# A two-layer decoder trunk on one Trainium2 core: the last down-weight sums of a layer are made behind the fourth product of pair 10 instead of behind pair 9

## The chip, the cores and the metric

The kernel runs on one core of one Trainium2 chip. Its time is the device time of one execution in microseconds (us), as the median of several runs. The engines of the core work side by side, each through its own queue in order: TensorE (PE, matrix products, with its weight loads as PEld), VectorE (DVE, elementwise work), ScalarE (ACT, elementwise work, casts, and it issues some transfers), GpSimd (POOL) and SyncE (SP, here only an issuer of transfers). They wait for one another through semaphores. [...]

## What is computed

A trunk of two layers on 512 tokens of width 1024. Layer one mixes tokens by pooling, layer two by differential attention; each is followed by a SwiGLU block with 2816 hidden columns, and both parts by a normalization:

```python
def _swiglu(x, w_gate, w_up, w_down):
    return (jax.nn.silu(x @ w_gate) * (x @ w_up)) @ w_down

    for i in range(DEPTH):
        ...
        x = _layernorm(ALPHA * x + h, ln_mix_g[i], ln_mix_b[i])
        x = _layernorm(ALPHA * x + _swiglu(x, w_gate[i], w_up[i], w_down[i]), ln_ffn_g[i], ln_ffn_b[i])
```

Only the SwiGLU block, which runs once in each layer (`ffn`, lines 570 to 1154), has to do with the change.

## The kernel before

**Precision.** Every matrix is split into a high part (a cast on ACT) and a low part (the rest, a subtraction on DVE), and a product is three matmuls: high by high, high by low, low by high. In the trace `g_65h` and `g_65l` are the two parts of a gate or up weight tile, `d_3h` and `d_3l` those of a down weight tile, and `raw` and `r` the tiles as loaded, before the split.

**Fewer products.** The hidden columns are taken in blocks of 128: 22 blocks, numbered so that block k and block k + 11 make pair k. For the pairs of the list `SPLIT` (2 to 10), gate and up are computed together by a fast scheme that needs seven products of half-size operands in place of eight (function `strassen`). Its products are named P1, Q5, P6, Q3, P7, P2 and Q4, and run in that order on TensorE, 24 matmuls each. They use three banks: A collects P1, P6, P7 and Q4, C collects Q5 and Q3, and B holds a copy of A after P1 and then collects P2. Between the products the banks are read:

- after P1, ACT copies A to B (L1015)
- after Q5, ACT copies C to the hidden tile `hid` (L1017); Q3 then adds into C, so it waits for that copy
- after P6, ACT copies A to `hid` (L1019); P7 then adds into A
- after Q3, DVE subtracts with C (L1024)
- after P7, DVE subtracts with A (L1026); Q4 then adds into A, so it waits for that subtraction
- after P2 and Q4, ACT takes the silu of B and A (L1042, L1031), and DVE multiplies (L1044, L1045)

**The down weights and their sums.** The down product is computed by the same kind of scheme, so it needs sums of blocks of the down weights. They are made ahead, one set of terms for each k from 0 to 10, while the pairs run. For a set of terms, POOL issues two loads (L823) and then a third load that accumulates onto the first (L824); this is `load_terms`. Later `weight_sums` makes two additions on DVE (L829, L830), and at the next `catch_up` two transfers issued on ACT (L834) store the four sums in the array `tsum` in memory. In the down product SP loads them back (`r<-tsum`, L612). The tile `b` is one of the buffers of these terms; `b_10` is that of the last set.

**What sets the order.** The program is written out in order; each engine runs its instructions in the order of the code. A unit of the list `ORDER` is a plain block (f) or a fast pair (p). Behind each product of a fast pair the code splits weights ahead of need (`ahead`), issues the stores of sums made earlier (`catch_up`), and then, if the tag of that product stands in the tuple `SUMMED`, makes the next set of sums (`weight_sums`). A tag without a product, such as `p9`, means behind the whole unit. So each of the eleven tags in `SUMMED` is the place of one set of sums, and the stores of a set are issued behind the product that comes next. Behind pair 10 comes the down product, whose items are cast and split on ACT and DVE in the gaps of pair 10. Lines 264 and 265 (`affine`) apply the scale and shift of the previous normalization to one block of `res`.

Of the kernel before, what the change touches and what calls it, by code (L numbers as in the profile page):

```python
# [49 lines left out]
EARLY = (1, 0)  # L50
PRE = SPLIT[:2]
SUMS = {1: (2, 1), 2: (2, 1)}
SUMMED = ("f1", "f2", "f3", "p3", "p4", "p5P2", "p6P7", "p7P7", "p8P6", "p9Q5", "p9")
EAGER = 6
GB = "p3"
MORE = True
# [22 lines left out]
def trunk(ctx, tc, x, wall, pscale, lam_p, subln, table, lng, lnb, band, first, onehot, out):  # L79
# [490 lines left out]
    def ffn(layer, late):  # L570
# [7 lines left out]
        with tc.tile_pool(name=f"ffn{layer}", bufs=1) as fp:  # L578
# [264 lines left out]
            def weight_sums():  # L843
                g = sum_terms(summed_rows[0])
                summed_rows[0] += 1
                next(g)
                behind.append(g)
# [4 lines left out]
            def catch_up():  # L852
                for g in list(behind):
                    if next(g, g) is g:
                        behind.remove(g)
# [139 lines left out]
            def strassen(k):  # L995
# [10 lines left out]
                for p in BEGUN if begun else GATE:  # L1006
# [30 lines left out]
                    if not (k == PRE[0] and p == "Q5"):  # L1037
                        catch_up()
                    if f"p{k}{p}" in SUMMED:
                        weight_sums()  # L1040
# [7 lines left out]
            for kind, i in units(layer):  # L1048
                (plain if kind == "f" else strassen)(i)
                unit = f"{kind}{i}"  # L1050
                if unit in SUMMED:
                    weight_sums()
# [636 lines left out]
```

## Time and profile before

| | us |
|---|---|
| median of 3 runs | 935.93 |
| the runs | 937.68, 929.84, 935.93 |
| the profiled execution's own time | 932.08 |
| its span, first to last instruction | 930.3 |

The profile has the span and the busy time of each engine, the waits (which instruction waited for which), the chain of work that ended last, and timelines. A row of a timeline gives the start in us from the span's start, the duration in us, the engine, the line of the kernel, the operation, the tiles it writes and reads, and, in brackets, the idle time of the engine ahead of it and what ended it. ACTq and SPq are the queues of ACT and SP where they issue transfers. A matmul is recorded with its start; the ends are modelled and overlap the next start, so the pace of a product is read from the starts. The granted clock of TensorE was 0.998 of full speed in this execution.

### The profile page before, as it was taken

To read this page: it belongs to the slowest core of one execution; us is meant where nothing else is said; L and a number is where in the kernel's file an instruction comes from. 1 tells how busy PE (TensorE), PEld (TensorE's weight loads), DVE (VectorE), ACT (ScalarE), POOL (GpSimd) and SP (SyncE) were. 2 spreads that over 40 slices of the span, in tenths; PEclk is the share of its full clock that TensorE was granted. 3 is DMA by queue.
4 is the path that set the end of the run, shared out by engine and by line. 5 is a ranking of instruction groups with operands and counts; after the bars stand their busy time and mean duration, and the time that the engine had idled before them with its cause. 6 is when DMAs were issued, how large, how long until landed. Compare 5 with 4: busy or idle time off the path is not lost. (4 is left out here: it accounts for less than half of the span.)

```text
span 930.3 us, 15038 instructions
## 1 busy us (share of the span) xinstructions
PE 917.7 (99%) x5806; PEld 826.9 (89%) x5806; DVE 803.9 (86%) x1163; ACT 529.0 (57%) x841; POOL 110.4 (12%) x129
## 2 busy tenths in 40 slices
PE   9999999999999999999999999999999999999996
PEld 8999999999988888878888888989999999988885
DVE  7998798998889998868989786877798999889988
ACT  6773354544555557676878854843454444555551
POOL 4121121110100001201111100201111110100001
PEclk9999999999999999999999999999999999999999
DMA  8397888877656688976664622468878887756653
GB/s 222 130 296 227 291 253 248 261 248 236 219 194 201 193 238 236 226 194 163 158 148 113 156 92 72 158 227 259 263 195 291 266 262 226 229 185 204 192 204 102
DMA packets 72518, 192.50 MB, mean 207 GB/s; under 512 B 14548, under 2 KB 14804, under 8 KB 72446
## 3 DMA queue, kind: packets, MB, share of 16 engines
q1 hardware_dynamic: 44572, 121.36, 39.6%
q0 software_dynamic: 15712, 46.93, 22.4%
q10 hardware_dynamic: 12162, 23.25, 6.7%
q8 instruction: 45, 0.74, 0.3%
q14 instruction: 27, 0.22, 0.1%
HBM read 166.33 MB, written 25.19 MB: 206 GB/s over the span
## 5 line engine op out<-in xcount | busy, mean ns | idle before, releaser
L713 DVE TENSOR_TENSOR raw<-raw,raw 128x1024 f32<-128x1024 f32 x52 | 63.3, 1221 | 0.7
L160 DVE TENSOR_TENSOR xs<-hid,xs 128x512 fp32r<-128x512 f32 x84 | 53.5, 639 | 0.0
L159 ACT CAST xs<-hid 128x512 fp32r<-128x512 f32 x84 | 48.6, 581 | 0.4 <-DVE hid L1044 0.4
L1322 ACT ACTIVATE p<-p,mn 128x128 f32<-128x128 f32 (+3 forms) x64 | 35.3, 552 | 14.1 <-DVE mn L1317 14.1
L823 POOL DMA_DIRECT2D b<-in_wall x24 | 17.9, 793 | 141.5 <-DMA tsum<-b 35.1
L1317 DVE CUSTOM_DVE_ANT_0 p<-s,bias 128x128 f32<-128x128 f32 (+3 forms) x64 | 28.0, 485 | 1.1 <-PE s L1302 1.1
L823 POOL DMA_DIRECT2D hid<-in_wall x20 | 15.0, 751 | 114.0 <-DVE hid L829 28.6
L1017 ACT COPY hid<-C 128x512 f32<-128x512 f32 x18 | 10.6, 587 | 29.1 <-PE C L919 14.3
L1024 DVE TENSOR_TENSOR hid<-C,hid 128x512 f32<-128x512 f32 x18 | 12.4, 690 | 16.4 <-PE C L919 13.4
L235 POOL TENSOR_TENSOR rs<-rs,mhalf 128x1 f32<-128x1 f32 x16 | 12.5, 782 | 102.7 <-DVE rs L234 95.7
L286 ACT ACTIVATE y<-pt,bT,gT 128x128 f32<-128x128 f32 x40 | 15.0, 455 | 15.9 <-PE pt L272 15.8
L226 DVE BATCH_NORM_STATS2 st<-res 128x6 f32<-128x512 f32 x32 | 22.2, 694 | 1.1
L1019 ACT COPY hid<-A 128x512 f32<-128x512 f32 x18 | 10.6, 586 | 20.4 <-PE A L919 20.4
L824 POOL DMA_DIRECT2D b<-in_wall x12 | 14.8, 1230 | 59.7 <-DMA b<-in_wall 59.7
L1031 ACT ACTIVATE sg<-A 128x512 f32<-128x512 f32 x18 | 10.7, 596 | 19.0 <-PE A L919 19.0
L1026 DVE TENSOR_TENSOR hid<-hid,A 128x512 f32<-128x512 f32 x18 | 12.3, 681 | 10.6 <-PE A L919 10.6
L1336 DVE SCALAR_TENSOR_TENSOR p<-p,sm,p 128x128 f32<-128x128 f32 (+3 forms) x32 | 17.6, 552 | 1.1
L713 DVE TENSOR_TENSOR more<-more,raw 128x1024 f32<-128x1024 f32 x15 | 18.3, 1220 | 0.2
L1042 ACT ACTIVATE sg<-B 128x512 f32<-128x512 f32 x14 | 8.3, 593 | 15.3 <-DVE hid L830 6.2
L265 DVE TENSOR_TENSOR res<-res,gb 128x512 f32<-128x512 f32 (+1 forms) x20 | 16.0, 799 | 0.7
L777 ACT CAST xs<-hid 128x1024 fp32r<-128x1024 f32 x8 | 8.4, 1052 | 14.3 <-DVE hid L786 8.7
L160 POOL TENSOR_TENSOR sql<-sq,sqh 128x512 fp32r<-128x512 f32 x7 | 9.3, 1325 | 60.5 <-ACT sqh L159 60.5
(1237 smaller groups left out, 3590.6 us busy)
## 6 DMA issues: line engine op xcount, KB each, us to landing
raw<-in_wall SPq DMA_DIRECT2D x120, 512.0 KB, 5.7
r<-tsum SPq DMA_DIRECT2D x40, 512.0 KB, 4.0
b<-in_wall POOLq DMA_DIRECT2D x36, 512.0 KB, 6.3
hid<-in_wall POOLq DMA_DIRECT2D x30, 512.0 KB, 6.1
r<-in_wall SPq DMA_DIRECT2D x30, 512.0 KB, 4.0
tsum<-b ACTq DMA_DIRECT2D x24, 512.0 KB, 3.8
tsum<-hid ACTq DMA_DIRECT2D x20, 512.0 KB, 5.6
more<-in_wall SPq DMA_DIRECT2D x10, 512.0 KB, 7.0
```

Source lines behind the costliest of these rows:

```text
L159: nc.scalar.copy(dst_h, src)
L160: (low or nc.vector).tensor_tensor(dst_l, src, dst_h.bitcast(F32), op=ALU.subtract)
L226: nc.vector.bn_stats(stats[n, s][:, d, :], res[:, s, d * 512 : (d + 1) * 512])
L235: nc.gpsimd.tensor_tensor(rs, rs, mhalf, op=ALU.pow)
L265: nc.vector.tensor_tensor(z, z, gb[:, 1, c], op=ALU.add)
L286: nc.scalar.activation(y[:, k, :], pt[:, k * P : (k + 1) * P], AF.Identity, bias=bT[:, n, kk : kk + 1], scale=gT[:, n, kk : kk + 1],)
L713: tt(t, raws[pair[0]], raws[pair[1]], op=ALU.add)
L823: nc.gpsimd.dma_start(out=t[:, j], in_=src[:, j])
L824: nc.gpsimd.dma_start(out=t[:, 0], in_=src[:, :, 1], accum_op=ALU.add)
L1317: nc.vector.tensor_tensor_reduce(out=p, in0=accs[c], in1=biases[h][:, w - 1 :: -1] if w < S else biases[h][:, ::-1], op0=ALU.add, op1=ALU. ...
L1322: nc.scalar.activation(p, p, AF.Exp, bias=mn[:, q, c : c + 1], scale=-1.0, accum_out=sm[:, q, c : c + 1],)
L1336: nc.vector.scalar_tensor_tensor(p0[:, r], p0[:, r], sm[:, q, 0:1], p1[:, r], op0=ALU.mult, op1=ALU.add)
```

## The change

One tag of the tuple `SUMMED` is another: the eleventh set of sums (the one of `b_10`) is made behind the product Q3 of pair 10, the fourth of its seven, in place of behind pair 9. The change acts in both layers.

```diff
 EARLY = (1, 0)
 PRE = SPLIT[:2]
 SUMS = {1: (2, 1), 2: (2, 1)}
-SUMMED = ("f1", "f2", "f3", "p3", "p4", "p5P2", "p6P7", "p7P7", "p8P6", "p9Q5", "p9")
+SUMMED = ("f1", "f2", "f3", "p3", "p4", "p5P2", "p6P7", "p7P7", "p8P6", "p9Q5", "p10Q3")
 EAGER = 6
 GB = "p3"
 MORE = True
```

The instructions on each engine are the same in number and kind. On DVE, at the border of pair 9 and pair 10 in the first layer (the numbers behind the names are those of buffers), the row before was:

```order
 L850 TENSOR_TENSOR hid_534<-hid_534 128x256
-L829 TENSOR_TENSOR b_10_2642<-b_10_2642 128x512
-L830 TENSOR_TENSOR b_10_2642<-b_10_2642 128x512
 L264 TENSOR_TENSOR res<-res,gb_1386 128x512
 L265 TENSOR_TENSOR res<-res,gb_1386 128x512
```

The two sums no longer stand between the last work of pair 9 (L850) and the scale and shift of `res`. On DVE in pair 10 of the same layer, the row now is, from the subtraction with bank C behind Q3:

```order
L1024 TENSOR_TENSOR hid_534<-C_10_2782,hid_534 128x2x256 [waits PE_49]
L160 TENSOR_TENSOR d_1l<-r_1_2713,d_1h 128x1024 [waits DMAHW1_49,Activation_49]
L160 TENSOR_TENSOR xs_535<-hid_534,xs_535 128x512 [waits Activation_49]
L829 TENSOR_TENSOR b_10_2642<-b_10_2642 128x512 [waits DMAHW0_49,DMAHW6_49,DMASW7_49,DMASW0_49]
L830 TENSOR_TENSOR b_10_2642<-b_10_2642 128x512 [waits DVE_49]
L1026 TENSOR_TENSOR hid_534<-hid_534,A_10_2781 128x2x256 [waits PE_49]
L160 TENSOR_TENSOR d_2l<-r_2_2808,d_2h 128x1024 [waits DMAHW2_49,Activation_49]
```

They stand there ahead of the subtraction with bank A (L1026); before, L1026 followed the split of `xs` directly. On ACT, the row before, from the copy of bank A to B behind P1 of pair 10:

```order
L1015 COPY B_3_679<-A_10_2783 128x512 [waits PE_49,Activation_49]
L834 DMA tsum_536<-b_10_2642 128x2x512 [waits DMAHW3_49,DMASW0_49]
L834 DMA tsum_536<-b_10_2642 128x2x512 [waits DMASW7_49,DVE_49]
L1017 COPY hid_534<-C_10_2784 128x2x256 [waits PE_49]
L1019 COPY hid_534<-A_10_2783 128x2x256 [waits PE_49]
```

and on ACT now, from the same copy on:

```order
L1015 COPY B_3_679<-A_10_2781 128x512 [waits PE_49,Activation_49]
L1017 COPY hid_534<-C_10_2782 128x2x256 [waits PE_49]
L1019 COPY hid_534<-A_10_2781 128x2x256 [waits PE_49]
L159 CAST d_0h<-r_0_2637 128x1024 [waits DMAHW7_49]
L159 CAST xs_535<-hid_534 128x512
L159 CAST d_1h<-r_1_2713 128x1024 [waits DMAHW1_49]
L159 CAST xs_535<-hid_534 128x512
L159 CAST d_2h<-r_2_2808 128x1024 [waits DMAHW2_49,PE_49]
L159 CAST xs_535<-hid_534 128x512
L834 DMA tsum_536<-b_10_2642 128x2x512 [waits DMAHW6_49,DMASW0_49]
L834 DMA tsum_536<-b_10_2642 128x2x512 [waits DMAHW0_49,DMASW7_49,DVE_49]
L159 CAST d_3h<-r_3_2836 128x1024 [waits DMAHW3_49,PE_49]
```

The two stores moved from ahead of the copy of bank C (L1017) to behind the casts for the third down item, ahead of the cast of `d_3h`; the second of them waits for the sums on DVE.

## The prediction

> **What bounds the kernel now.** I read the page first, then the waits of TensorE, then the chain of work that ended last, and at the place that the chain names the timelines of TensorE, DVE and ACT.
>
> The page's head and the row of its part 1 (busy us, share of the span, instructions):
>
> ```profile
> span 930.3 us, 15038 instructions
> PE 917.7 (99%) x5806; PEld 826.9 (89%) x5806; DVE 803.9 (86%) x1163; ACT 529.0 (57%) x841; POOL 110.4 (12%) x129
> ```
>
> TensorE is the bound nearly everywhere: 930.3 - 917.7 = 12.6 us of the span are without a matmul. A change that leaves the matmuls alone can win only from those. The waits of TensorE (us in total, times, the longest) and of its weight loads say what the idle time in the middle waits for:
>
> ```profile
> PE C L919 <- ACT hid L1017: 2.6, 2, 1.7
> PE pt L272 <- DVE res L244: 0.2, 1, 0.2
> ```
> ```profile
> PEld C L919 <- ACT hid L1017: 3.0, 2, 1.9
> ```
>
> There is one wait of size, twice, once in each layer: a matmul into bank C waits for the copy of bank C by ACT (L1017). The matmuls on either side, from TensorE's timeline (start us, us, operation; idle time before and its releaser in brackets), first layer then second:
>
> ```profile
> 248.48 0.28 PE L919 MATMUL A<-xs,g_66l 128*128 128x256 f32 x1
> 250.45 0.50 PE L919 MATMUL C<-xs,g_67h 128*128 128x256 f32 x2 [1.69 <-ACT hid L1017]
> 250.79 0.28 PE L919 MATMUL C<-xs,g_67l 128*128 128x256 f32 x1
> 804.81 0.28 PE L919 MATMUL A<-xs,g_66l 128*128 128x256 f32 x1
> 806.02 0.50 PE L919 MATMUL C<-xs,g_67h 128*128 128x256 f32 x2 [0.93 <-ACT hid L1017]
> 806.36 0.28 PE L919 MATMUL C<-xs,g_67l 128*128 128x256 f32 x1
> ```
>
> g_66 is the third product of pair 10 (P6), g_67 the fourth (Q3). Why the copy is late stands in the chain of work that ended last (start us, us, what):
>
> ```profile
> 796.89 6.55 DMA b<-in_wall
> ...
> 803.52 0.70 DVE b L829
> ...
> 804.25 0.70 DVE b L830
> ...
> 804.97 0.37 ACTq L834
> ...
> 805.38 0.59 ACT hid L1017
> ...
> 806.02 3.13 PE C L919 x24
> 809.15 2.88 PE A L919 x24
> ...
> 877.66 45.02 PE P L1079 x198
> ```
>
> Read downwards: the accumulating transfer of the last down-weight terms lands at 803.44; the two sums (L829, L830) come after it; the store of the sums (L834) is issued on ACT's queue after them; ACT's copy of bank C stands behind that store; TensorE waits for the copy. A product is 24 matmuls in 2.88 us, 0.12 each. From 806 on the chain is TensorE alone to the last normalization. So these sums, with nothing urgent about them, hold TensorE in each layer.
>
> **The change part by part.** Nothing is added or removed: two sums on DVE and two stores on ACT go from ahead of pair 10 to behind its fourth product, in both layers.
>
> *What the old place gives back.* Layer one: the Q3 matmul was due at 248.48 + 0.12 = 248.60 and started at 250.45, 1.85 late; its first two took 250.79 - 250.45 = 0.34 where 0.24 is the pace, 0.10 more. Layer two: due at 804.93, started at 806.02, 1.09, and again 0.10. Sum 1.95 + 1.19 = 3.14 us. [...]
>
> I take 3.14, from starts, since a start is recorded and an end is modelled; the ends for the range are 2.6 and 3.2.
>
> *Is the copy then in time?* It needs only bank C's product Q5 (ended 802.2 by the pace) and TensorE needs it at 804.93. The store, the only thing that held it, is gone: slack some 2 us.
>
> *What the sums cost in the new place.* Now they stand on DVE just ahead of L1026 (the subtraction that reads bank A after P7), and the first Q4 matmul, which writes into bank A again, waits for L1026. That is the one place where the change can lose, so I laid out DVE and ACT there with the rows of layer two (layer one first, for the same wait; then DVE, then ACT):
>
> ```profile
> 247.95 0.69 DVE L829 TENSOR_TENSOR b<-b 128x512 f32<-128x512 f32 x1 [3.95 <-DMA b<-in_wall]
> ```
> ```profile
> 799.91 0.42 DVE L850 TENSOR_TENSOR hid<-hid 128x256 f32<-128x256 f32 x1
> 803.52 0.69 DVE L829 TENSOR_TENSOR b<-b 128x512 f32<-128x512 f32 x1 [3.19 <-DMA b<-in_wall]
> ...
> 804.86 0.68 DVE L264 TENSOR_TENSOR res<-res,gb 128x512 f32<-128x512 f32 x1
> ...
> 807.32 1.22 DVE L719 TENSOR_TENSOR g_70l<-raw,g_70h 128x1024 fp32r<-128x1024 f32 x1
> 808.46 1.22 DVE L160 TENSOR_TENSOR d_0l<-r,d_0h 128x1024 fp32r<-128x1024 f32 x1
> ...
> 810.20 0.68 DVE L1024 TENSOR_TENSOR hid<-C,hid 128x512 f32<-128x512 f32 x1
> 810.80 1.22 DVE L160 TENSOR_TENSOR d_1l<-r,d_1h 128x1024 fp32r<-128x1024 f32 x1
> ...
> 812.53 0.68 DVE L1026 TENSOR_TENSOR hid<-hid,A 128x512 f32<-128x512 f32 x1
> ```
> ```profile
> 805.86 0.59 ACT L1019 COPY hid<-A 128x512 f32<-128x512 f32 x1
> 806.34 1.06 ACT L159 CAST d_0h<-r 128x1024 fp32r<-128x1024 f32 x1
> ...
> 809.27 1.06 ACT L159 CAST d_2h<-r 128x1024 fp32r<-128x1024 f32 x1
> ...
> 811.95 1.05 ACT L159 CAST d_3h<-r 128x1024 fp32r<-128x1024 f32 x1 [1.10 <-PE A L919]
> ```
>
> DVE after L850 goes straight on: L264 at about 800.25, and g_70l ends (807.32 + 1.22 - 804.86 = 3.68 later) at 803.9. It then waits for d_0h. On ACT, L1019 comes after P6's last matmul ends, 804.81 + 0.28 = 805.09, so at 805.13; d_0h 0.48 behind it at 805.61, ended 806.67. DVE then keeps its old distances: d_0l 806.70, L1024 1.74 later at 808.44, d_1l at 809.04, and 1.73 behind it, at 810.77, the place of L1026. There the sums go in: L829 and L830 take up 804.86 - 803.52 = 1.34, so L1026 runs from 812.11 to 812.79. TensorE, unheld, starts Q4 at 804.93 + 3 x 2.88 = 813.57. Slack 0.78 us, and the same in layer one, whose rows have the same distances from Q3 on. So L1026 costs nothing while that slack stands; if it is gone, each us beyond it is lost once in each layer. Bounds: 0 and, had the sums their whole 1.34 us uncovered, 1.34 - 0.78 = 0.56 a layer. I take 0, nearest to the rows.
>
> *Will the accumulated terms be there?* The landing row of L824's transfers, SP's row of the loads that read the sums, the sixth of them alone, and the landing row of L834's stores:
>
> ```profile
> DMA to landing us min/median/max: 5.7/7.3/12.9
> ```
> ```profile
> 812.04 18.08 SPq L612 DMA_DIRECT2D r<-tsum  x8
> ```
> ```profile
> 824.66 0.32 SPq L612 DMA_DIRECT2D r<-tsum  x1
> ```
> ```profile
> DMA to landing us min/median/max: 2.8/4.0/11.2
> ```
>
> Issued at 796.89, the slowest of its kind (12.9) would land at 809.8, before 810.77; the one seen took 6.55. Wait gone.
>
> *The stores on ACT.* The first waits for nothing that is late and is issued behind d_2's two casts, near 810.1; the second waits for L830, until 812.2, and takes 0.37. d_3h stands behind it: 812.6 in place of 811.95 less the gain, some 1.8 us later against TensorE. Its user is the fourth item of the down products: they start at 813.57 + 2.88 = 816.45, an item has 12 matmuls of 45.02 / 198 = 0.227, so 816.45 + 3 x 2.73 = 824.6. Ten us of cover. Behind it on ACT stand the two silus: the first could run at 813.8 and runs behind d_3's casts at 814.1, the second waits for Q4 as before. 0.
>
> *The stores and who reads them.* The first read of the last terms is the sixth of the loads from tsum, 824.66 less the gain of 1.19, 823.5; the first store, issued at 810.1, lands at 814 by the median and at 821.3 by the worst. Were it held even so, its user is the twelfth item, some 30 us behind 816.45. 0.
>
> *The loads on SP.* Slots free earlier, since g_69l and g_70l run about 4.6 us earlier: two loads of down weights go out earlier. None is late. POOL's queue holds nothing behind the terms but work of the next stage. 0.
>
> Sum: 932.08 - 3.14 = 928.94 for the profiled execution, 0.34%.
>
> **Rivals.**
>
> *Q4 takes over part of the wait.* L1026 late by more than 0.78 us holds TensorE one product later. For it: ACT and DVE are only 0.8 us ahead there, with a chain of casts ahead of both. Against it: each row of that chain has a fixed length. Were L1026 late by 1.5 us, each layer would lose 0.7: 930.4.
>
> *The gain of layer one does not reach the end.* Between the layers stand the attention and its normalizations, where a transfer could set the pace. For it: the same place in layer two comes 555 us later. Against it: TensorE has only one idle row there, 0.2 us. It would give 932.08 - 1.19 = 930.9.
>
> *The moved stores crowd the down-weight loads.* The stores now run beside the loads that feed the down products. [...] By rows: the slowest store takes 11.2 where 4.0 is usual; loads as late, 7.2 us, still fall within the ten us of cover. Beyond that the gain of both layers is eaten: 932.
>
> *Slower.* The one mechanism: the accumulate lands so late that DVE holds L829 in the new place, with L1026 and then Q4 behind it, in place of Q3. It decides from where Q4 loses more than 3.14 over both layers: landing after 810.77 + 0.78 + 1.19 = 812.7 in layer two, 15.9 us after issue, where 12.9 is the most seen. At 20 us, L829 would start at 816.89 and L1026 end 2.02 later, 5.3 behind Q4's time; twice that less 3.14 is 7.5 more than before: 939.5.
>
> **How the numbers follow.** Full gain 0.70; Q4 takes part 0.12; layer one's gain lost 0.08; stores crowd loads 0.05; slower 0.05. The runs shown differ by more than the change: 929.84, 935.93, 937.68 and the profiled 932.08, mean 933.88. The profiled execution is 3.85 below the median, so I set the gain against the mean of the four: 933.88 - 3.14 = 930.7. The range runs from the fastest run with the full gain, 929.84 - 3.14 = 926.7, to the median with none, 936.0. Faster or slower by over 1% (about what a measurement of this kernel can tell from no change) means under 926.6 or over 945.3: the full gain reaches the first only on a run faster than any shown, 0.05; the slower rival reaches the second only at (9.4 + 3.1) / 2 = 6.3 us a layer, 0.03; within 1%, 0.92.
>
> **What would show it.** Right: no wait of TensorE on L1017; no wait of DVE on the terms' transfer at L829; the rows A, C, A of pair 10 at 0.12 through; TensorE's busy time the same and the span shorter by about 3 us; Q4 at once behind P2, with L1026 ended some 0.8 us before it. Wrong: an idle row at the first Q4 matmul of pair 10 with DVE's L1026 as releaser, an idle row in the first down products with ACT or DVE casts, or new idle time in the attention.

## The result, and the profile after

The changed kernel takes 928.3 us (median of 7 runs, 927.45 to 928.78); the kernel before, now with 7 runs, 935.93 (929.84 to 937.68). The ratio on record is 0.993, with a 95% interval from 0.9903 to 0.9956 (the two medians alone would give 0.992). Two things stand out: the gain of the medians, 7.6 us, is more than twice the 3.14 that the sum gave for the profiled execution, and more than the 5.2 between the median before and the 930.7 that was forecast; and the runs, which lay 7.8 us apart before, now lie 1.3 apart.

The head and the first row of the page of the changed kernel:

```profile
span 926.5 us, 15034 instructions
PE 916.4 (99%) x5806; PEld 826.6 (89%) x5806; DVE 804.0 (87%) x1163; ACT 529.2 (57%) x841; POOL 110.3 (12%) x129
```

All that TensorE still waits for in the changed kernel (us in total, times, the longest):

```profile
PE warm L392 <- POOL ident masks.py:199: 1.9, 1, 1.9
PE pool L441 <- ACT fh L159: 0.2, 1, 0.2
PE pt L272 <- DVE res L244: 0.2, 1, 0.2
```

The wait for ACT's copy of bank C (L1017) has gone. In TensorE's timeline, layer one, the last P6 matmul and the first of Q3:

```profile
248.16 0.28 PE L919 MATMUL A<-xs,g_66l 128*128 128x256 f32 x1
248.28 0.40 PE L919 MATMUL C<-xs,g_67h 128*128 128x256 f32 x2
```

Q3 starts at the pace, 0.12 later, where 1.97 passed before. The new place of the sums on DVE, layer two:

```profile
804.12 1.23 DVE L160 TENSOR_TENSOR d_0l<-r,d_0h 128x1024 fp32r<-128x1024 f32 x1 [2.76 <-ACT d_0h L159]
...
808.20 0.69 DVE L829 TENSOR_TENSOR b<-b 128x512 f32<-128x512 f32 x1
808.92 0.69 DVE L830 TENSOR_TENSOR b<-b 128x512 f32<-128x512 f32 x1
809.53 0.68 DVE L1026 TENSOR_TENSOR hid<-hid,A 128x512 f32<-128x512 f32 x1
```

L829 follows its predecessor without a wait. L1026 ends at 810.21; the first Q4 matmul, which waits for it, starts at 802.24 + 0.12 + 3 x 2.88 = 811.00, so 0.79 us of cover. For layer one the two rows themselves, DVE's and TensorE's:

```profile
255.46 0.68 DVE L1026 TENSOR_TENSOR hid<-hid,A 128x512 f32<-128x512 f32 x1
```
```profile
256.92 0.40 PE L919 MATMUL A<-xt,g_70h 128*128 128x256 f32 x2
```

256.92 - 256.14 = 0.78, the cover that was forecast. The same stretch on ACT, layer two:

```profile
799.67 0.59 ACT L1017 COPY hid<-C 128x512 f32<-128x512 f32 x1 [1.42 <-PE C L919]
802.55 0.59 ACT L1019 COPY hid<-A 128x512 f32<-128x512 f32 x1 [2.29 <-PE A L919]
...
805.38 0.43 ACTq L834 DMA_DIRECT2D tsum<-b  x1
...
809.64 0.37 ACTq L834 DMA_DIRECT2D tsum<-b  x1
810.11 1.05 ACT L159 CAST d_3h<-r 128x1024 fp32r<-128x1024 f32 x1 [2.56 <-DVE b L830]
```

Both copies now wait for nothing but their product. The second store still waits for the sums and holds d_3h by 2.56 us, and nobody waits for d_3h.

### The profile page after: what moved, and what is told of

Read it like the earlier page. It is cut to its first block, busy times and chain, and to the rows that moved or that the text cites. A ratio compares the mean times of both kernels' runs of the same rounds, so it can differ in the third digit from the quotient of the medians.

```text
span 926.5 us, 15034 instructions
## 1 busy us (share of the span) xinstructions
PE 916.4 (99%) x5806; PEld 826.6 (89%) x5806; DVE 804.0 (87%) x1163; ACT 529.2 (57%) x841; POOL 110.3 (12%) x129
## 5 line engine op out<-in xcount | busy, mean ns | idle before, releaser
L1017 ACT COPY hid<-C 128x512 f32<-128x512 f32 x18 | 10.6, 588 | 22.2 <-PE C L919 17.2
L1026 DVE TENSOR_TENSOR hid<-hid,A 128x512 f32<-128x512 f32 x18 | 12.3, 682 | 10.6 <-PE A L919 10.6
L265 DVE TENSOR_TENSOR res<-res,gb 128x512 f32<-128x512 f32 (+1 forms) x20 | 16.0, 799 | 0.7
L264 DVE TENSOR_TENSOR res<-res,gb 128x512 f32<-128x512 f32 (+1 forms) x20 | 15.8, 791 | 0.0
```

Source lines behind the costliest of these rows:

```text
L264: nc.vector.tensor_tensor(z, z, gb[:, 0, c], op=ALU.mult)
L265: nc.vector.tensor_tensor(z, z, gb[:, 1, c], op=ALU.add)
```

## The experiments

My theory was that the place is harmless, and that what it cost was the wait for a late transfer, passed on by ACT's queue (store in front of copy) to TensorE. What the forecast left open was why the gain is 7.6 and not 3.1.

**Is the rest the same wait, only longer?** Three more executions of the kernel before, unchanged (no edit) and each with a profile, and six of the changed one on the same chip.

> The kernel before once more, unchanged, for its profile. My theory: in the runs of before that are slower than the profiled 932.08, the accumulating transfer of the last down-weight terms (L824 of b_10) lands later, DVE waits longer at L829, the store on ACT waits longer, and TensorE waits longer at the first Q3 matmul of pair 10. Then the time is about 928.3 plus the loss at that matmul summed over both layers (3.14 in the profile shown), within 0.7 us. Rival: the slower runs lose time elsewhere (start, attention, down products), and the loss at Q3 stays near 3.1 while the time varies by several us.

> As look_a, a second execution of the kernel before: time = 928.3 plus the loss at the two first Q3 matmuls of pair 10, within 0.7 us (theory); the loss stays near 3.1 us and does not follow the time (rival).

> As look_a, a third execution of the kernel before: time = 928.3 plus the loss at the two first Q3 matmuls of pair 10, within 0.7 us (theory); the loss stays near 3.1 us and does not follow the time (rival).

> The changed kernel once more, on the same chip as the three looks at the kernel before, in five rounds. Theory: 928.3 within 1 us in every run, spread under 2 us, since TensorE waits for no transfer any more; ratio to before 0.990 to 0.997, depending on how late the transfer lands in the runs of before. Rival (the gain of 0.7% was chance of the runs shown): ratio 0.997 and a spread as wide as before's.

The three executions took 936.34, 935.66 and 935.78 us. The changed kernel again took 928.12 (927.26 to 929.36) against 937.25 of before on that chip (932.09 to 940.01, 11 runs), ratio 0.9906 (0.9879 to 0.9932). Its runs lie 2.1 us apart, a little wider than the 2 expected, where those of before lie 7.9 apart. In look_c, layer one, DVE and then TensorE:

```profile
250.45 0.69 DVE L829 TENSOR_TENSOR b<-b 128x512 f32<-128x512 f32 x1 [7.32 <-DMA b<-in_wall]
```
```profile
252.95 0.80 PE L919 MATMUL C<-xs,g_67h 128*128 128x256 f32 x2 [5.07 <-ACT hid L1017]
```

DVE waits 7.32 us where the profile of before had 3.95, and TensorE idles 5.07 in place of 1.69. Then something adds to it: two matmuls take 0.80 where they took 0.50. The stretches around the gap in that execution (columns: the stretch, its length, busy us and count of PE, PEld, DVE, ACT and POOL, the granted clock of TensorE, DMA share, GB/s):

```profile
244.00:248.00 4.00, 3.88 (x33) 3.67 (x31) 0.00 (x0) 0.00 (x0) 0.00 (x0) 1.00 0.93 219
248.00:252.00 4.00, 0.00 (x0) 0.00 (x0) 1.52 (x3) 0.00 (x0) 0.00 (x0) 0.86 0.32 91
252.00:256.00 4.00, 3.05 (x14) 3.06 (x15) 3.97 (x5) 3.69 (x6) 0.00 (x0) 0.50 0.61 210
256.00:260.00 4.00, 4.00 (x29) 4.00 (x29) 3.00 (x5) 1.88 (x3) 0.00 (x0) 0.79 0.90 275
260.00:264.00 4.00, 4.00 (x36) 4.00 (x35) 3.56 (x6) 1.57 (x2) 0.00 (x0) 1.00 0.55 175
```

After the gap the granted clock is halved for another 4.75 us (until 257.70), so the gap costs more than its idle time. The whole loss is best read as the distance from the last P6 matmul of pair 10 to the first matmul of the down product, by starts, in each layer; where nothing holds TensorE it is 11.64 us.

| execution | time | layer one | layer two | lost in both | time less loss |
|---|---|---|---|---|---|
| changed kernel | 928.30 | 11.64 | 11.64 | 0 | 928.3 |
| after_again | 928.26 | 11.64 | 11.64 | 0 | 928.3 |
| before, as shown ahead | 932.08 | 13.58 | 12.82 | 3.1 | 929.0 |
| look_a | 936.34 | 15.10 | 16.02 | 7.8 | 928.5 |
| look_b | 935.66 | 17.36 | 13.59 | 7.7 | 928.0 |
| look_c | 935.78 | 19.03 | 12.37 | 8.1 | 927.7 |

Less the loss, every execution of the kernel before lies within 0.7 us of the changed kernel's time: within that, the wait and what follows from it are the whole difference. The same table read by idle time alone (5.85, 5.86 and 5.54 us in the last three) would leave 1.8 to 2.6 us unexplained. Of that, 0.5 is 0.26 at each gap: the modelled end of the matmul ahead lies 0.28 behind its start where the pace is 0.12, and the first two matmuls behind the gap take 0.34 in place of 0.24. The rest is the halved clock.

In the four experiments that follow, the kernel before, run beside them, took 935.02 us (929.91 to 941.33, 31 runs), and the ratios are to it.

**Is it the store on ACT, or DVE's own wait?** The sums stay where they were, only the stores are held back to where the changed kernel has them.

```diff
-                    if not (k == PRE[0] and p == "Q5"):
+                    if not (k == PRE[0] and p == "Q5") and not (k == HALF - 1 and p in ("P1", "Q5", "P6", "Q3")):
                         catch_up()
```

> The sums stay at their old place on DVE, behind pair 9; only their two stores on ACT are held back until behind the fifth product of pair 10, where the changed kernel has them. Theory (the store in front of the copy of bank C on ACT's queue is what held TensorE): no wait of TensorE at Q3. What is left is DVE's own wait at L829, which pushes L1026: with the transfer landing as in the profile of before L1026 ends 0.4 us ahead of Q4, so no loss, 928 to 929; with a landing 2 us later Q4 loses up to 1.9 us a layer, 932. So ratio 0.992 to 0.996, and any idle row of TensorE stands at Q4 with L1026, not at Q3. Rival (DVE's wait itself held TensorE at Q3): the idle row at Q3 stays and the time is that of before.

932.12 us (928.85 to 935.5, 12 runs), ratio 0.9964 (0.9938 to 0.9989). In its profile, layer one, DVE and TensorE:

```profile
250.24 0.69 DVE L829 TENSOR_TENSOR b<-b 128x512 f32<-128x512 f32 x1 [7.23 <-DMA b<-in_wall]
...
259.24 0.68 DVE L1026 TENSOR_TENSOR hid<-hid,A 128x512 f32<-128x512 f32 x1
```
```profile
247.49 0.28 PE L919 MATMUL A<-xs,g_66l 128*128 128x256 f32 x1
247.60 0.40 PE L919 MATMUL C<-xs,g_67h 128*128 128x256 f32 x2
...
259.98 0.50 PE L919 MATMUL A<-xt,g_70h 128*128 128x256 f32 x2 [2.92 <-DVE hid L1026]
```

With a transfer as late as in look_c (7.2 us of DVE's wait), TensorE no longer stops at Q3 but at Q4, for L1026, as the theory said. So the store in front of the copy was what held Q3. But DVE's wait is not free either: it comes out three products later. The ratio lies just above the expected 0.992 to 0.996. Layer one lost 5.3 us, more than the 1.9 expected of a landing 2 us later: DVE waited 3.3 us longer than in the profile shown ahead, the clock was halved behind the gap, and a small idle row at P2 (0.41 us, on the split of g_69 that DVE's wait pushed) was not foreseen. In layer two of the same profile the distance is 11.64, no loss.

**One product later.** The last sums behind P1 of pair 10, so that the stores stand between the copies of C and A on ACT.

```diff
-SUMMED = ("f1", "f2", "f3", "p3", "p4", "p5P2", "p6P7", "p7P7", "p8P6", "p9Q5", "p9")
+SUMMED = ("f1", "f2", "f3", "p3", "p4", "p5P2", "p6P7", "p7P7", "p8P6", "p9Q5", "p10P1")
```

> The sums are made behind the first product of pair 10 in place of behind pair 9, so the stores are issued one product later, behind the copy of bank C on ACT (L1017) and ahead of the copy of bank A (L1019). DVE still waits for the transfer at L829. Theory: the position of the stores against L1017 decides; the copy is in time, TensorE does not wait at Q3, 928.0 to 929.5, ratio 0.992 to 0.995. Rival (the late transfer and DVE's wait cost by themselves, wherever ACT's stores stand): an idle row of TensorE at P7 or Q4 of about the old size, time within 1 us of before.

929.61 us (927.52 to 931.28, 12 runs), ratio 0.9933 (0.991 to 0.9957); the median is 0.1 above the expected band. ACT in layer one, and TensorE:

```profile
249.51 1.82 ACTq L834 DMA_DIRECT2D tsum<-b  x2
251.37 0.58 ACT L1019 COPY hid<-A 128x512 f32<-128x512 f32 x1 [5.15 <-PE C L919]
```
```profile
252.01 0.50 PE L919 MATMUL A<-xs,g_68h 128*128 128x256 f32 x2 [0.66 <-ACT hid L1019]
```

Now the store holds the next copy and P7 behind it, by 0.66 us. (The copy's bracket names a product of bank C, but the copy starts at 251.37, 0.04 behind the end of the two stores' issue at 249.51 + 1.82 = 251.33.) One product (2.88 us) more of distance takes most of the loss away, but not on every run: the order on ACT decided which product paid (Q3 by 1.69 us before, P7 by 0.66 here), the lateness how much.

**Take the lateness away and leave the place.** The set before the last is summed earlier, behind pair 8, so that the loads of the last set start earlier; the last sums stay behind pair 9.

```diff
-SUMMED = ("f1", "f2", "f3", "p3", "p4", "p5P2", "p6P7", "p7P7", "p8P6", "p9Q5", "p9")
+SUMMED = ("f1", "f2", "f3", "p3", "p4", "p5P2", "p6P7", "p7P7", "p8P6", "p8", "p9")
```

> Sums and stores of the last set stay at the old place, behind pair 9; but the set before it is summed and stored some 3 us earlier (behind pair 8 in place of behind the second product of pair 9), so that the loads of the last set start some 3 us earlier. Theory (the place is harmless, the lateness of the transfer at that place is the cost): the transfer lands near 800 in place of 803.4, the copy of bank C ends before TensorE needs it, 928 to 930, ratio 0.992 to 0.996. Rival (the sums and stores cost at that place even when their data is there, by their own time on DVE and ACT): the loss at Q3 stays above 1 us in all.

928.04 us (927.62 to 928.64, 8 runs), ratio 0.9921 (0.9891 to 0.9951): the whole gain, and runs as close together as those of the changed kernel, with the sums and stores at the place that the change left. In its timelines, layer one, POOL's accumulating load and the sums on DVE:

```profile
233.94 1.22 POOL L824 DMA_DIRECT2D b<-in_wall  x1 [4.35 <-DMA b<-in_wall]
```
```profile
242.34 0.68 DVE L829 TENSOR_TENSOR b<-b 128x512 f32<-128x512 f32 x1
```

The load is issued at 233.94, not the 3 but 6 us earlier than in the profiled kernel before (240.30), and L829 waits for nothing. Sums and stores at the old place cost TensorE nothing when their data is there (11.64 us in both layers of this profile). The rival falls.

**How much cover has the new place?** The changed kernel with three DVE instructions more behind the last sums:

```diff
                 tt(t[:, 1, 0], t[:, 1, 1], t[:, 1, 0], op=ALU.add)
+                for _ in range(3 if k == HALF - 1 else 0):
+                    tt(t[:, 1, 0], t[:, 1, 0], t[:, 1, 0], op=ALU.max)
```

> The changed kernel with three more DVE instructions of 0.7 us behind the last sums (each takes the maximum of a sum with itself, which alters nothing), some 2.1 us in front of L1026 in each layer. It measures the cover that the prediction gave, 0.78 us. Theory: TensorE waits at the first Q4 matmul of pair 10 for L1026, 2.1 - 0.8 + 0.1 = 1.4 to 1.5 us a layer, 931.2 in all (ratio 1.003 to the changed kernel). Rival (that place has more cover, or L1026 does not hold Q4): 928.3, no idle row.

931.33 us (930.47 to 932.47, 12 runs), ratio 0.9958 (0.9934 to 0.9983), and 1.003 to the changed kernel's 928.3. DVE and TensorE in layer one (the added lines shift L1026 to L1028):

```profile
255.38 2.14 DVE L832 TENSOR_TENSOR b<-b 128x512 f32<-128x512 f32 x3
257.44 0.68 DVE L1028 TENSOR_TENSOR hid<-hid,A 128x512 f32<-128x512 f32 x1
```
```profile
258.18 0.50 PE L921 MATMUL A<-xt,g_70h 128*128 128x256 f32 x2 [1.28 <-DVE hid L1028]
```

Each layer's distance is 13.18, so 1.54 lost, against 1.4 to 1.5 expected. Of the 2.1 us of delay 0.8 are covered; the rest, 1.28 us, is idle time of TensorE, and 0.26 come on top as at the other gaps.

The remaining executions, in the columns of the table above:

| execution | time | layer one | layer two | lost in both | time less loss |
|---|---|---|---|---|---|
| held_stores | 932.83 | 16.94 | 11.64 | 5.3 | 927.5 |
| sums_p10P1 | 929.34 | 12.55 | 11.63 | 0.9 | 928.4 |
| early_terms | 927.64 | 11.64 | 11.64 | 0 | 927.6 |
| late_sums | 931.05 | 13.18 | 13.18 | 3.1 | 928.0 |

Less the loss, all ten lie between 927.5 and 929.0. No version tried is clearly faster than the changed kernel; the one with the earlier loads is equal to it (928.04 beside 928.12 and 928.3).

## Why the prediction was right or wrong

- *The wait and its chain* (transfer, sums, store, copy, matmul): right, and shown by its parts: with the transfer earlier it goes, with the store moved it shifts to another product.
- *The gain against the profiled execution*: 928.94 was worked out, 928.3 measured. The starts place the other 0.6 elsewhere: 0.3 lies ahead of pair 10 of layer one, where the last P6 matmul starts at 248.16 against 248.48, and 0.3 between the two stretches of pair 10, where the lead grows from 2.27 to 2.57 us. TensorE's busy time, which was to stay the same, fell by 1.3 us (917.7 to 916.4): of the 3.14, 0.52 stood in it and not in the idle rows, as the 0.26 at each gap.
- *Full gain, Q4 not held*: right, the cover read from the trace is the 0.78 us that was laid out, and with 2.1 us of added work the loss comes out at Q4 as that cover has it.
- *Layer one's gain reaches the end*: right; the changed execution has no new idle row in the attention.
- *The stores and loads crowd nothing*: right, no wait of TensorE on a down weight. The first store went out at 805.38; the 810.1 laid out is 807.5 in this execution, which runs 2.57 us earlier there, so it went 2.2 us ahead of that and had no one to hold. The row read as the landing of L834's stores (median 4.0) counts the loads from `tsum` too; for the stores alone the median is 4.9, with the same 2.8 and 11.2 at the ends, which leaves the cover as it was.
- *How the gain stands to the median*: this step failed. The text found the profiled execution 3.85 below the median, treated that as scatter apart from the wait, and set the gain against the mean of the four executions: 930.7. The three further executions show that the scatter of the kernel before was the wait itself, 3.1 us lost in the profiled execution and 7.7 to 8.1 in executions near the median. So what the wait costs differs from run to run while the time without it does not; 928.94 was the better forecast for every run, and the gain on the median 7.6 and not 5.2.
- *The price of an idle gap*: its length and 0.10 us for the first two matmuls were counted, which was all of it in the profiled execution. In each of the three further ones a second term comes in, the halved clock behind one of the two gaps, 1.3 to 2.1 us.
- *The ends and limits laid out beside the sum*: of its ends 2.6 and 3.2, the first is TensorE's idle rows, the second stands in no run; by starts 3.1 was lost. The bound of 0.56 a layer counts the sums' 1.34 us twice, since the 0.78 is what is left with them in. And 812.7 is the landing from which layer two alone would lose more than before; for 3.14 over both layers it is 1.57 a layer, 813.1. None of the three entered the time.

That the range held the time owes to its lower end, which came from the fastest run with the full gain, and that end is partly luck: less the loss every execution lies at 927.5 or above, so the run of 929.84 can hardly have lost more than 2.3 us to the wait, and 3.14 could not have been won from it. Not settled is why the transfer lands so differently: in layer one of look_a, look_b and look_c it was issued at 240.28, 243.28 and 241.31 and DVE got it at 249.25, 249.44 and 250.45. Both the issue and the time to land vary, and no run here took them apart.

## What to carry to other kernels

Where a late transfer is waited for in front of other work in an engine's queue, the runs can scatter as the transfer does, as they did here (7.8 us apart before, 1.3 after); a profile shows one draw of that wait (DVE's at L829 in layer one was 3.95, 5.46, 6.40 and 7.32 us in the four profiles of the kernel before). So when one execution lies off the median, first ask whether the wait in question is what varies, and forecast the time without it rather than subtract it from an average. The cure can be either end: move the waiting work to a place with cover, whose size can be read from the next instruction that TensorE needs, or start the transfer earlier.

## What the runs showed of the hardware that was not expected

**The clock was halved behind some gaps of a few microseconds and not behind others.** In layer two of look_a, TensorE idled 2.65 us, ran at full pace for another 0.8 us, and then at half clock for 3.4 us (the columns are those of the stretches above):

```profile
808.94 0.50 PE L919 MATMUL C<-xs,g_67h 128*128 128x256 f32 x2 [2.65 <-ACT hid L1017]
```
```profile
806.00:809.00 3.00, 0.35 (x4) 0.15 (x2) 2.49 (x4) 0.70 (x2) 0.00 (x0) 1.00 0.53 199
809.00:810.00 1.00, 1.00 (x8) 1.00 (x9) 1.00 (x2) 1.00 (x2) 0.00 (x0) 0.88 0.99 383
810.00:813.00 3.00, 3.00 (x16) 3.00 (x16) 3.00 (x4) 2.30 (x4) 0.00 (x0) 0.50 0.59 184
813.00:814.00 1.00, 1.00 (x10) 1.00 (x9) 0.59 (x2) 0.51 (x1) 0.00 (x0) 0.92 0.84 266
```

In layer one of the same execution a longer gap, 3.20 us, left the clock at 1.00 (246.55 to 253.38), and that layer's distance, 15.10, holds beside the 11.64 only the gap and 0.26. The gap of 2.92 us in held_stores was followed by half clock too (0.50 from 262 to 264), as were those of 4.15 us in look_b (0.50 from 252 to 255) and 5.07 us in look_c (0.50 from 252 to 256). In the profiled kernel before, the clock stayed at 1.00 behind both gaps (1.69 and 0.93 us), and in every other layer whose one gap was of up to 1.7 us the distance holds the gap and 0.24 to 0.26 us, which leaves nothing for a halved clock. So the length alone did not decide: 2.65 us was followed by half clock where 3.20 us was not. What did decide was not shown: no run here moved such a gap by itself.

**A store on ACT went out ahead of casts that stand before it.** In the changed kernel the first store, behind d_2's casts in the code, was issued at 805.38, while d_1's cast (804.50 to 805.55) was still running:

```profile
804.50 1.05 ACT L159 CAST d_1h<-r 128x1024 fp32r<-128x1024 f32 x1
805.38 0.43 ACTq L834 DMA_DIRECT2D tsum<-b  x1
805.45 0.62 ACT L159 CAST xs<-hid 128x512 fp32r<-128x512 f32 x1
805.97 1.05 ACT L159 CAST d_2h<-r 128x1024 fp32r<-128x1024 f32 x1
```

In this trace the store that had to wait for the sums held the cast behind it (d_3h, 2.56 us); the one that need not wait went out ahead of three casts that the code has before it.
